# A decoder layer's first projection: two token groups of v and a taken from x without its norm, and the first loads reordered

## Chip, cores and metric

The kernel runs on one core of a Trainium2 chip. The metric is device time in microseconds; a time is the median of several executions. One execution was also taken with the hardware profiler, and all rows shown here come from it.

## The reference, cut to what matters

One layer of a decoder over 512 tokens of 1024 features, all in float32:

```python
h = rms_norm(x, g_mix)                 # x * rsqrt(mean(x*x) + eps) * g
proj = h @ w_in                        # (512, 1024) @ (1024, 3088)
q, k, v, g, a_low, B, C, u = split(proj)    # 256, 256, 512, 512, 16, 512, 512, 512 columns
...                                    # gated linear attention, short convolution
x = x + concat(A, B) @ w_out
x = x + hier_moe(rms_norm(x, g_moe))   # 16 experts, two of them per token
x = x + sigmoid(rms_norm(x, g_ple) @ w_ple_gate) * (p @ w_ple_proj)
return rms_norm(x, g_final)
```

What matters here is the product that gives v (512 columns) and a_low (16 columns). The norm divides each row of x by one number, so `rms_norm(x) @ w` equals `r * ((x * g) @ w)`, where r is that row's reciprocal root mean square: the factor may be applied to the rows of the product.

## The kernel before, in words

**Precision.** A float32 product is made of three products of rounded operands. A matrix is split into a high part (`hi`, `hTh`), rounded by ScalarE (ACT) as it copies, and a low part (`lo`, `hTl`), the remainder, formed by VectorE (DVE). TensorE (PE) then adds up high x high, high x low and low x high. So each weight tile and each tile of activations passes ACT, then DVE, before its last matmul.

**Weights.** `Stream` (line 53) keeps a list of weight blocks to be loaded (`specs`), a few load buffers (`raw0` to `raw2` here), and split tiles. `load` (line 83) issues the DMAs of the next block on SyncE's queue (SP) where a buffer is free. `split` (line 103) queues the high parts on ACT (line 117, scaled by the gain g_mix, which comes as the columns of `cst`) and the low parts on DVE (line 118); with `later=True` the low parts are handed back as a function and are queued where that is called. `give` frees the buffer when the last low part is queued, and that queues the next load. One block has 512 rows of w_in as four k tiles of 128 rows. The blocks for v and a have 528 columns, 512 wide ones and 16 narrow ones, which are two DMAs.

**Work of the first stage.** Tokens are four groups (t) of 128; features are eight k tiles of 128, in two halves (i) of four. Per group: `norm_in(t)` (line 328) squares half 0 on ACT and half 1 on DVE, adds them on DVE, and takes the power -0.5 on GpSimd (POOL), line 238; `scale_in(t)` (line 332) multiplies half 0 on ACT and half 1 on DVE by the result; `tr_half(t, i)` (line 337) transposes four 128 x 128 blocks on PE into PSUM (line 341), copies them to `hTh` on ACT (line 344), and forms `hTl` on DVE (line 345); `va_mm` (line 373) runs six matmuls of 264 columns per k tile (line 378); `va_out` (line 381) copies v and a out of PSUM on ACT and DVE. The next stage, the q|k projection (`proj_steps`, line 442, matmuls on line 454), reads `hTh` and `hTl` of all four groups.

**Order.** The schedule is written out by hand: each engine runs its instructions in the order in which the Python code queues them, and waits at the head of its queue for what it needs. Before the stage, dummy matmuls (`warm`, line 314) run on PE. Lines 400 to 440 are the order of the stage; in it group 0 is normed, scaled and transposed before its first matmul:

```python
    norm_in(0)
    copy_cst()
    scale_in(0)
    tr_half(0, 0)()
    W.pump(1)
```

**Loads.** SP issues x of group 0 (two halves of 256 KB), then the first weight block in two parts (each 512 KB wide and 8 KB narrow, shown as 16.0 KB by the profile), x of group 1, the second block likewise, x of groups 2 and 3, small rows, and the third block. g_mix is loaded on ACT's queue.

Of the kernel before, what the change touches and what calls it, by code (L numbers as in the profile page):

```python
# [13 lines left out]
AF = mybir.ActivationFunctionType  # L14
OP = mybir.AluOpType
# [6 lines left out]
NT = S // P  # L22
NK = D // P
# [29 lines left out]
class Stream:  # L53
# [26 lines left out]
            self.free.append(at)  # L80
        self.load()

    def load(self, n=99, parts=1, eng=None):
        eng = eng or self.nc.sync
        while n and self.free and self.specs:
            n -= 1
            spec = self.specs.pop(0)
            if callable(spec):
                spec()
                continue  # L90
            src, r0, nk, c0, cn, c1, c1n, gain = spec
            w = cn + c1n
            at, raw = self.slot(nk * w)
            v = raw.rearrange("p (k c) -> p k c", k=nk)
            rows = src[r0:r0 + nk * P, :].rearrange("(k p) c -> p k c", p=P)
            for i in range(parts):
                ks = slice(nk // parts * i, nk // parts * (i + 1))
                eng.dma_start(v[:, ks, :cn], rows[:, ks, c0:c0 + cn])
                if c1n:
                    eng.dma_start(v[:, ks, cn:], rows[:, ks, c1:c1 + c1n])  # L100
            self.loaded += [(raw, nk // 2, w, 0, None, gain), (raw, nk // 2, w, 1, at, gain)]

    def split(self, hi=None, lo=None, eng=None, later=False):
        eng = eng or self.nc.vector
        raw, n, w, i, at, gain = self.loaded.pop(0)
        if hi is None:
            hi = self.hl.tile([P, n * w], F32R, tag="hi", name="hi")
            lo = self.hl.tile([P, n * w], F32R, tag="lo", name="lo")
        rw = raw[:, n * w * i:n * w * (i + 1)]
        los = []  # L110
        if gain is None:
            self.nc.scalar.copy(hi, rw)  # L112
            los.append(lambda: eng.tensor_sub(lo, rw, hi.bitcast(F32)))  # L113
        else:
            for j in range(n):
                c_, g_ = slice(j * w, (j + 1) * w), gain[:, n * i + j:n * i + j + 1]
                self.nc.scalar.activation(hi[:, c_], rw[:, c_], AF.Copy, scale=g_)  # L117
                los.append(lambda c_=c_, g_=g_: eng.scalar_tensor_tensor(  # L118
                    lo[:, c_], rw[:, c_], g_, hi[:, c_].bitcast(F32), op0=OP.mult, op1=OP.subtract))
        self.ready.append([(hi[:, j * w:(j + 1) * w], lo[:, j * w:(j + 1) * w]) for j in range(n)])  # L120

        def rest(n=9):
            for _ in range(min(n, len(los))):
                los.pop(0)()
            if not los and at is not None:
                self.give(at)

        if later:
            self.live += 1
            return rest  # L130
        rest()

    def pump(self, n=1, eng=None):
# [18 lines left out]
def hymba_layer(ctx, tc, x, p, g_mix, w_in, w_gla_gate, b_gla_gate, g_gla_out, w_conv, w_out,  # L152
# [3 lines left out]
    x, out = x[0], out[0]  # L156
    p, w_in, w_out = p[0, 0], w_in[0], w_out[0]
    ve, se, pe, ge, sy = nc.vector, nc.scalar, nc.tensor, nc.gpsimd, nc.sync
    ctx.enter_context(tc.manual_schedule())

    def pool(stack, name, bufs, **kw):
        return stack.enter_context(tc.tile_pool(name=name, bufs=bufs, **kw))
# [3 lines left out]
    ring = pool(ctx, "ring", 1)  # L166
# [7 lines left out]
    def mm_ps(name):  # L174
        return ps.tile([P, HALF], F32, tag="mm", name=name)

    def aux_ps(name):
        return psa.tile([P, HALF], F32, tag="aux", name=name)

    def half(i):  # L180
        return slice(i * HALF, (i + 1) * HALF)

    def tok(t):
        return slice(t * P, (t + 1) * P)


    W = Stream(nc, hlp, 6)
# [8 lines left out]
    def X(t):  # L196
        return xt[t // 2][:, (t % 2) * D:(t % 2 + 1) * D]

    ident = consts.tile([P, P], F32, name="ident")
# [4 lines left out]
    cst = consts.tile([P, 40], F32, name="cst")  # L204
# [3 lines left out]
    later = consts.tile([P, 5, 4, 4], U8, name="later")  # L208
# [44 lines left out]
    def t2k(name, dt=F32):  # L253
        return t2.tile([P, HALF], dt, tag="t2", name=name)

    def txk(name, dt=F32):
        return tx.tile([P, HALF], dt, tag="tx", name=name)
# [8 lines left out]
    for ci in range(2):  # L266
        add_columns(w_out, HALF * ci)

    def load_x(t):
        for i in range(2):  # L270
            sy.dma_start(X(t)[:, half(i)], x[tok(t), half(i)])

    load_x(0)
    rows = t2k("rows")[:, :P]
    wg = mc.tile([RANK, 256], F32, name="wg")
    ve.memset(rows, 0.0)
# [1 line left out]
    def load_row(eng, r0, vec):  # L278
        n = vec.shape[-1] // P
        eng.dma_start(rows[r0:r0 + n, :], vec[0].rearrange("(k p) -> k p", p=P))  # L280

    load_row(se, 0, g_mix)
    se.preload_act_table_set("natural_log_exp_and_others")
    W.free += [(ring, f"raw{i}") for i in range(3)]
    W.load(1, 2)
    load_x(1)
    W.load(1, 2)
    load_x(2)
    load_x(3)
    for r0, vec in ((8, b_gla_gate), (10, g_gla_out), (23, g_moe), (31, g_ple)):  # L290
        load_row(sy, r0, vec)
    sy.dma_start(rows[11:23, :], w_conv[0].rearrange("j (i p) -> (j i) p", p=P))
# [7 lines left out]
    def small_loads():  # L300
        ge.dma_start(wr[:, :, 0:4], w_group[0].rearrange("(k p) c -> p k c", p=P))
        ge.dma_start(wr[:, :, 4:20], w_router[0].rearrange("(k p) c -> p k c", p=P))
        bcast(brt[:, 0:4], b_group[0], 4)
        bcast(brt[:, 4:20], b_router[0], 16)
        bcast(gmoe, g_moe[0], D)
# [3 lines left out]
    def make_cst(a, b_):  # L309
        pt = aux_ps(f"pt_rows{a}")  # L310
        pe.transpose(pt[:, :b_], rows[:b_, :], ident[:b_, :b_])
        return lambda: se.copy(cst[:, a:b_], pt[:, a:b_])

    def warm(n, pw):

        for _ in range(n):
            pe.matmul(pw[:, :P], ones, ones, start=True, stop=True)

    pw = mm_ps("pw")

    def fold_gain():
        for k in range(NK):
            ge.tensor_scalar(wr[:, k, :], wr[:, k, :], cst[:, 23 + k:24 + k], None, op0=OP.mult)


    xn, rin = {}, {}

    def norm_in(t):
        xn[t] = junk = [txk(f"xn{t}_{i}") for i in range(2)]
        rin[t] = norm_rows(X(t)[:, :], junk, f"mix{t}")  # L330

    def scale_in(t):
        junk, r = xn[t], rin[t]
        se.mul(junk[0], X(t)[:, half(0)], r)
        ve.tensor_scalar(junk[1], X(t)[:, half(1)], r, None, op0=OP.mult)

    def tr_half(t, i):

        pk = aux_ps(f"pk{t}_{i}")
        for k in range(4):  # L340
            pe.transpose(pk[:, tok(k)], xn[t][i][:, tok(k)], ident)
        pv = pk.rearrange("p (k t) -> p k t", k=4)
        dh, dl = hTh[:, 4 * i:4 * i + 4, tok(t)], hTl[:, 4 * i:4 * i + 4, tok(t)]
        se.copy(dh, pv)
        return lambda: ve.tensor_sub(dl, pv, dh.bitcast(F32))

    def tr_in(t):
        for i in range(2):
            tr_half(t, i)()
# [21 lines left out]
    at_ = [mc.tile([P, RANK], F32, name=f"at{t}") for t in range(NT)]  # L371

    def va_mm(t, pp, ks):
        for k in ks:
            wh, wl = va[k]
            for n, (a, b_) in enumerate(((hTh, wh), (hTh, wl), (hTl, wh))):
                for i in range(2):
                    pe.matmul(pp[i][:, :264], a[:, k, tok(t)], b_[:, i * 264:(i + 1) * 264],
                              start=(k + n == 0), stop=(k == NK - 1 and n == 2))

    def va_out(t, pp):
        v_ = t2k(f"v{t}")
        ve.tensor_copy(at_[t], pp[1][:, 248:264])
        se.copy(v_[:, :264], pp[0][:, :264])
        ve.tensor_copy(v_[:, 264:], pp[1][:, :248])
        vt.append(v_)

    def a_tr(t, pa):
# [1 line left out]

    pp = {}

    def va_half(t, i):
        if i == 0:
            pp[t] = [mm_ps(f"va{t}_{j}") for j in range(2)]
        va_mm(t, pp[t], range(4 * i, 4 * i + 4))
        if i:
            va_out(t, pp[t])

    warm(6, pw)  # L400
    copy_cst = make_cst(0, 8)
    warm(6, pw)
    norm_in(0)
    copy_cst()
    scale_in(0)
    tr_half(0, 0)()
    W.pump(1)
    lo = W.split(later=True)
    lo(1)
    norm_in(1)  # L410
    lo(1)
    lo = tr_half(0, 1)
    scale_in(1)
    lo()
    va = W.take() + W.take()
    va_half(0, 0)
    tr_in(1)
    norm_in(2)
    va_half(1, 0)
    W.pump(1)  # L420
    scale_in(2)
    W.pump(1)
    va += W.take() + W.take()
    tr_in(2)
    va_half(0, 1)
    norm_in(3)
    scale_in(3)
    va_half(1, 1)
    tr_in(3)
    make_cst(8, 39)()  # L430
    small_loads()
    make_masks()
    va_half(2, 0)
    va_half(2, 1)
    fold_gain()
    W.pump(2)
    va_half(3, 0)
    va_half(3, 1)
    make_routing()
    W.done(4)  # L440

# [598 lines left out]
    t = NT - 1  # L1040
# [451 lines left out]
    for t in range(NT):  # L1492
        n = t + 1
# [15 lines left out]
    t = NT - 1  # L1509
# [29 lines left out]
    r = small.tile([P, 1], F32, tag="rstd", name="rs_last")  # L1539
# [33 lines left out]
```

## Time and profile before

| what | us |
|---|---|
| median of 3 runs | 609.72 (609.4 to 611.09) |
| the profiled execution, its own time | 609.15 |
| its span, first to last instruction | 607.4 |
| PE, DVE, ACT, POOL busy | 587.7, 481.6, 365.3, 113.6 |
| stage of v and a, first matmul to the q pass's first weight load | 8.76 to 38.84 |

Times in rows are microseconds from the span's start, durations of one instruction often in ns. PE is the matmul row, PEld the weight loads beside it. SPq and ACTq are DMA issues on those queues. L378 is line 378 of the kernel, and it may be a helper's line. A matmul's shown duration has its pipeline's length in it, so the pitch of a series is read from starts. An instruction's row says in brackets how long its engine was idle before it and what released it.

### The profile page before, as it was taken

The page shows a single profiled execution, that of the slowest core. Times are in us where ns is not written, and L with a number is a line of the kernel's source. Part 1 is how long each engine was busy: PE and PEld are TensorE (multiplying, and loading weights), DVE is VectorE, ACT ScalarE, POOL GpSimd, SP SyncE. Part 2 cuts the span into 40 slices and gives each one's busy share as a digit, 9 for nine tenths or more (in the row PEclk, how much of TensorE's full clock was granted, in tenths as well). Part 3 has the DMA queues.
Part 4 walks back from the last instruction along what each step waited for, and adds up shares of the span by engine and source line. Part 5 has one row for each costly group of instructions (what it writes and reads, how often), then busy time and mean ns, then how long its engine had stood idle before and what let it go on. Part 6 is the DMA issues. An engine that isn't in the chain of part 4 may idle for free.

```text
span 607.4 us, 8456 instructions
## 1 busy us (share of the span) xinstructions
PE 587.7 (97%) x3026; PEld 450.6 (74%) x3026; DVE 481.6 (79%) x814; ACT 365.3 (60%) x520; POOL 113.6 (19%) x148
## 2 busy tenths in 40 slices
PE   7999999999999999899999999999999999989995
PEld 6997888887687788677777777777777777666884
DVE  4742799874396476799999999999999999879764
ACT  5532537303715333768877878877787898776232
POOL 1440664100420000123210222220122210000101
PEclk9999999999999999999999999999999999999998
DMA  8732222221126958599999999999999999992001
GB/s 282 215 105 71 70 70 69 70 73 68 42 96 215 389 210 306 197 376 369 373 371 371 365 369 367 388 379 364 362 341 365 377 344 380 373 366 99 36 35 70
DMA packets 65324, 148.62 MB, mean 245 GB/s; under 512 B 4747, under 2 KB 5346, under 8 KB 65262
## 3 DMA queue, kind: packets, MB, share of 16 engines
q1 hardware_dynamic: 61374, 136.69, 60.9%
q0 software_dynamic: 3744, 11.09, 8.0%
q8 instruction: 24, 0.39, 0.3%
q10 hardware_dynamic: 160, 0.27, 0.1%
q14 instruction: 22, 0.18, 0.1%
HBM read 137.56 MB, written 12.71 MB: 247 GB/s over the span
## 4 chain that ended last, share of the span: by engine, by line
PE 52%; DVE 4%; ACT 2%; issue 1%; POOL 0%; DVEq 0%; POOLq 0%; ACTq 0%
PE pg L1125 14%; PE pd L1125 14%; PE pu L1125 13%; PE pgate L1125 5%; PE pt_xT L1113 2%; DVE lo L113 1%; PE pgate_last L1526 1%; PE pt_hT L1113 1%; DVE lo L118 1%; ACT hi L112 1%; PE px L1432 1%; PE pz L1260 0%; PE pslot L938 0%; ACT L1396 0%; ACT ye L1319 0%
## 5 line engine op out<-in xcount | busy, mean ns | idle before, releaser
L113 DVE TENSOR_TENSOR lo<-raw,hi 128x1024 fp32r<-128x1024 f32 x172 | 203.5, 1218 | 13.3 <-ACT hi L112 12.1
L112 ACT CAST hi<-raw 128x1024 fp32r<-128x1024 f32 x172 | 170.8, 1052 | 2.5 <-DMA raw<-in_w_exp_down_dram 1.7
L1095 POOL DMA_INDIRECT xe<-xgd,toki x16 | 27.0, 1685 | 190.5 <-PE pt_xT L1113 164.5
L118 DVE SCALAR_TENSOR_TENSOR lo<-raw,cst,hi 128x512 fp32r<-128x512 f32 (+1 forms) x56 | 44.7, 842 | 16.2 <-ACT hi L117 16.0
L113 DVE TENSOR_TENSOR lo<-x,hi 128x1024 fp32r<-128x1024 f32 x30 | 36.0, 1218 | 1.0 <-ACT hi L112 0.8
L117 ACT ACTIVATE hi<-raw,cst 128x512 fp32r<-128x512 f32 (+1 forms) x56 | 36.6, 717 | 0.0
L1146 POOL DMA_INDIRECT xd<-ye,rowi x15 | 22.9, 1525 | 48.6 <-ACT ye L1319 44.9
L112 ACT CAST hi<-x 128x1024 fp32r<-128x1024 f32 x30 | 30.9, 1052 | 0.0
L1125 PE MATMUL pg<-hi,xT_1h 128*96 128x512 f32 x60 | 24.3, 406 | 0.0
L1125 PE MATMUL pg<-hi,xT_0l 128*96 128x512 f32 x60 | 23.8, 396 | 0.0
L1125 PE MATMUL pg<-hi,xT_0h 128*96 128x512 f32 x60 | 23.8, 396 | 0.0
L1125 PE MATMUL pg<-lo,xT_0h 128*96 128x512 f32 x60 | 23.7, 395 | 0.0
L1125 PE MATMUL pg<-hi,xT_1l 128*96 128x512 f32 x60 | 23.6, 394 | 0.0
L1125 PE MATMUL pg<-lo,xT_1h 128*96 128x512 f32 x60 | 23.6, 393 | 0.0
L1125 PE MATMUL pu<-hi,xT_0h 128*96 128x512 f32 x56 | 22.7, 405 | 0.0
L1125 PE MATMUL pu<-hi,xT_1l 128*96 128x512 f32 x56 | 22.2, 396 | 0.0
L1125 PE MATMUL pu<-hi,xT_0l 128*96 128x512 f32 x56 | 22.2, 396 | 0.0
L1125 PE MATMUL pu<-hi,xT_1h 128*96 128x512 f32 x56 | 22.1, 394 | 0.0
L1125 PE MATMUL pu<-lo,xT_1h 128*96 128x512 f32 x56 | 22.1, 394 | 0.0
L1125 PE MATMUL pu<-lo,xT_0h 128*96 128x512 f32 x56 | 22.0, 393 | 0.0
L645 ACT ACTIVATE sq<-xs 128x512 f32<-128x512 f32 x4 | 2.5, 632 | 28.5 <-DVE xs L627 28.5
L737 POOL TENSOR_TENSOR xs<-xs,sg 128x128 f32<-128x128 f32 x16 | 11.3, 738 | 44.2 <-ACT sg L732 44.1
(584 smaller groups left out, 1588.6 us busy)
## 6 DMA issues: line engine op xcount, KB each, us to landing
raw<-in_w_exp_gate_dram SPq DMA_DIRECT2D x28, 1024.0 KB, 16.9
raw<-in_w_exp_down_dram SPq DMA_DIRECT2D x27, 1024.0 KB, 16.1
raw<-in_w_exp_up_dram SPq DMA_DIRECT2D x26, 1024.0 KB, 15.7
raw<-in_w_in_dram SPq DMA_DIRECT2D x10, 1024.0 KB, 5.0
x<-in_w_exp_up_dram SPq DMA_DIRECT2D x6, 1024.0 KB
x<-in_w_exp_down_dram SPq DMA_DIRECT2D x5, 1024.0 KB, 16.4
xs<-in_x_dram SPq DMA_DIRECT2D x16, 256.0 KB, 5.8
raw<-in_w_out_dram SPq DMA_DIRECT2D x4, 1024.0 KB
```

The costliest lines, as they stand in the source:

```text
L112: self.nc.scalar.copy(hi, rw)
L113: los.append(lambda: eng.tensor_sub(lo, rw, hi.bitcast(F32)))
L117: self.nc.scalar.activation(hi[:, c_], rw[:, c_], AF.Copy, scale=g_)
L118: los.append(lambda c_=c_, g_=g_: eng.scalar_tensor_tensor(lo[:, c_], rw[:, c_], g_, hi[:, c_].bitcast(F32), op0=OP.mult, op1=OP.subtract))
L645: se.activation(osq[c], to[c], AF.Square)
L737: ge.tensor_tensor(tv, tv, sgs[i][:, tok(t)], op=OP.mult)
L1095: ge.indirect_dma_start(out=x_, out_offset=None, in_=xgd, in_offset=bass.IndirectOffsetOnAxis(ap=idx, axis=0), bounds_check=S - 1, oob_is_ ...
L1113: pe.transpose(pt[:, k * n:(k + 1) * n], src[:n, tok(k)], ident[:n, :n])
L1125: pe.matmul(dst, a, b_, start=(k + n == 0), stop=(k == nk - 1 and n == 2))
L1146: ge.indirect_dma_start(out=xd, out_offset=bass.IndirectOffsetOnAxis(ap=idx, axis=0), in_=y_, in_offset=None, bounds_check=S + P - 1, oob_ ...
L1432: pe.transpose(pt[:, tok(k)], X(t)[:, ci * HALF + k * P:ci * HALF + (k + 1) * P], ident)
L1526: pe.matmul(pgl[i][:, :256], a, b_[:, 256 * i:256 * i + 256], start=(k + n == 0), stop=(k == NK - 1 and n == 2))
```

## The change

It has four parts.

1. For token groups 0 and 1, x itself is transposed (`tr_raw`), split, and multiplied with the gained weights. `va_out` multiplies the rows of v and a by r as it copies them out of PSUM. The normed and scaled groups 0 and 1 are still transposed later (`tr_in(0)`, `tr_in(1)`), since q, k and all other projections read them.
2. The two weight blocks are split k tile by k tile (`steps=True`: the high parts are handed back as functions too), and the order of matmuls is by k tile instead of by half (`va_k` for `va_half`).
3. The loads: x by halves, weights in four parts of 256 KB wide columns, the narrow columns of a block in two DMAs ahead of its wide ones; those of the first block on ACT's queue. Order on SP: x0 half 0, block 0, x1 half 0, x0 half 1, block 1, x1 half 1, groups 2 and 3, and then as before.
4. The copies of `cst` go from ACT to DVE. The dummy matmuls are eight before the first transposes and six after, for six and six. `make_cst(8, 39)`, `small_loads`, `make_masks` and `fold_gain` come later in the order.

The diff, cut:

```diff
     def load(..., narrow=None):
+            for n1 in range(2 * bool(c1n)):
+                ks = slice(nk // 2 * n1, nk // 2 * (n1 + 1))
+                (narrow or eng).dma_start(v[:, ks, cn:], rows[:, ks, c1:c1 + c1n])
             for i in range(parts):
                 eng.dma_start(v[:, ks, :cn], rows[:, ks, c0:c0 + cn])
-                if c1n:
-                    eng.dma_start(v[:, ks, cn:], rows[:, ks, c1:c1 + c1n])
...
-    W.load(1, 2)
-    load_x(1)
-    W.load(1, 2)
-    load_x(2)
-    load_x(3)
+    W.load(1, 4, narrow=se)
+    se.preload_act_table_set("natural_log_exp_and_others")
+    load_x(1, 0)
+    load_x(0, 1)
+    W.load(1, 4)
+    load_x(1, 1)
+    for t in range(2, NT):
+        for i in range(2):
+            load_x(t, i)
...
-        return lambda: se.copy(cst[:, a:b_], pt[:, a:b_])
+        return lambda: ve.tensor_copy(cst[:, a:b_], pt[:, a:b_])
...
+    def tr_raw(t, i):
+        return tr_half(t, i, X(t)[:, half(i)])
...
     def va_out(t, pp):
+        if t < 2:
+            r = rin[t]
+            ve.tensor_scalar(at_[t], pp[1][:, 248:264], r, None, op0=OP.mult)
+            se.mul(v_[:, :264], pp[0][:, :264], r)
+            ve.tensor_scalar(v_[:, 264:], pp[1][:, :248], r, None, op0=OP.mult)
...
+    warm(8, pw)
+    xlo = tr_raw(0, 0)
+    copy_cst = make_cst(0, 8)
+    copy_cst()
     warm(6, pw)
+    xlo()
+    (h0, l0), (h1, l1) = W.split(steps=True), W.split(steps=True)
+    va = W.take() + W.take()
+    for f in h0 + h1:
+        f()
+    l0(1)
+    va_k(0, 0)
+    l0(1)
+    va_k(0, 1)
+    xlo = tr_raw(1, 0)
+    l1(1)
+    va_k(0, 2)
+    xlo()
+    va_k(1, 0)
+    l1(1)
+    va_k(1, 1)
+    va_k(0, 3)
+    xlo = tr_raw(0, 1)
+    va_k(1, 2)
+    (h0, l0), (h1, l1) = W.split(steps=True), W.split(steps=True)
+    va += W.take() + W.take()
+    for f in h0:
+        f()
+    xlo()
+    l0(1)
+    va_k(1, 3)
+    l0(1)
+    va_k(0, 4, 5)
+    xlo = tr_raw(1, 1)
+    for f in h1:
+        f()
+    xlo()
+    l1(1)
+    norm_in(0)
+    va_k(0, 6)
+    va_k(1, 4)
+    l1(1)
+    va_k(1, 5)
+    va_k(0, 7)
+    norm_in(1)
+    va_k(1, 6)
+    norm_in(2)
+    va_k(1, 7)
+    scale_in(2)
+    tr_in(2)
+    scale_in(0)
+    va_k(2, 0, 1, 2)
+    norm_in(3)
+    tr_in(0)
+    scale_in(3)
+    va_k(2, 3, 4)
+    scale_in(1)
+    make_cst(8, 39)()
+    tr_in(3)
+    small_loads()
+    va_k(2, 5, 6, 7)
+    tr_in(1)
     make_masks()
     fold_gain()
+    va_k(3, 0, 1)
     W.pump(2)
+    va_k(3, 2, 3, 4, 5, 6, 7)
     make_routing()
```

## Rows read from the trace of the kernel before

**Rows 1.** The page, part 1: busy time, share of the span, instructions of PE.

```profile
PE 587.7 (97%) x3026; PEld 450.6 (74%) x3026; DVE 481.6 (79%) x814; ACT 365.3 (60%) x520; POOL 113.6 (19%) x148
```

**Rows 2.** Windows: stretch and length, busy us of each engine, PEclk, DMA, GB/s.

```profile
8.76:38.84 30.08, 27.98 (x217) 26.36 (x217) 19.55 (x48) 15.61 (x31) 14.18 (x41) 1.00 0.62 201
...
38.84:60.00 21.16, 21.16 (x89) 15.46 (x88) 6.54 (x11) 5.99 (x11) 0.00 (x0) 1.00 0.28 96
```

**Rows 3.** Timeline of PE in the head: start, us, instruction, idle before.

```profile
1.27 2.93 PE L317 MATMUL pw<-ones 128*128 128x128 f32 x12 [1.27 <-DVE ones L297]
...
2.07 1.06 PE L317 MATMUL pw<-ones 128*128 128x128 f32 x4
...
2.92 1.06 PE L317 MATMUL pw<-ones 128*128 128x128 f32 x4
...
8.76 0.51 PE L378 MATMUL va<-hi,hTh 128*128 128x264 f32 x2 [0.87 <-ACT hi L117]
...
19.09 1.09 PE L341 MATMUL pk<-ident,xn 128*128 128x128 f32 x8 [0.69 <-ACT xn L334]
...
19.94 0.49 PE L378 MATMUL va<-hi,hTh 128*128 128x264 f32 x2
...
27.17 0.51 PE L378 MATMUL va<-hi,hTh 128*128 128x264 f32 x2
...
38.84 0.19 PEld L454 LDWEIGHTS qk<-hTh,hi 128*128 128x128 f32 x1
```

**Rows 4.** Timeline of ACT, DVE and PE: the links of the chains.

```profile
7.97 2.62 ACT L117 ACTIVATE hi<-raw,cst 128x528 fp32r<-128x528 f32 x4
...
8.74 2.13 DVE L118 SCALAR_TENSOR_TENSOR lo<-raw,cst,hi 128x528 fp32r<-128x528 f32 x3
...
9.57 0.50 PE L378 MATMUL va<-lo,hTh 128*128 128x264 f32 x2 [0.29 <-DVE lo L118]
...
10.49 0.62 ACT L232 ACTIVATE xn<-xs 128x512 f32<-128x512 f32 x1
...
11.59 0.16 DVE L236 SCALAR_TENSOR_TENSOR msmix<-s2mix 128x1 f32<-128x1 f32 x1
...
12.88 0.72 ACT L334 ACTIVATE xn<-xs,rsmix 128x512 f32<-128x512 f32 x1 [1.21 <-POOL rsmix L238]
...
13.66 1.09 PE L341 MATMUL pk<-ident,xn 128*128 128x128 f32 x8 [0.41 <-ACT xn L334]
...
14.35 1.07 ACT L344 CAST hTh<-pk 128x512 fp32r<-128x512 f32 x2 [0.75 <-PE pk L341]
...
14.97 1.29 DVE L345 TENSOR_TENSOR hTl<-pk,hTh 128x512 fp32r<-128x512 f32 x2 [1.00 <-ACT hTh L344]
...
23.03 0.38 ACT L384 COPY v<-va 128x264 f32<-128x264 f32 x1 [1.78 <-PE va L378]
```

**Rows 5.** Loads: issues, first uses of x, SP's wait, issue to landing of x1.

```profile
1.10 0.59 ACTq L280 DMA_DIRECT2D rows<-in_g_mix_dram  x1
...
3.52 0.63 ACT L232 ACTIVATE xn<-xs 128x512 f32<-128x512 f32 x1 [0.52 <-DMA xs<-in_x_dram]
...
3.73 1.23 SPq L271 DMA_DIRECT2D xs<-in_x_dram  x2
...
4.30 0.69 DVE L233 SCALAR_TENSOR_TENSOR xn<-xs 128x512 f32<-128x512 f32 x1 [3.09 <-DMA xs<-in_x_dram]
...
6.96 0.37 SPq L98 DMA_DIRECT2D raw<-in_w_in_dram  x1
...
SPq L98 <- DMA raw<-in_w_in_dram: 0.7, 1, 0.7
...
xs<-in_x_dram SPq DMA_DIRECT2D x2, 256.0 KB, 5.8
```

**Rows 6.** Windows at the kernel's end: PE has no more work, then PEclk.

```profile
600.00:602.60 2.60, 0.00 (x0) 0.00 (x0) 1.44 (x5) 0.47 (x1) 0.39 (x1) 1.00 0.00 0
602.60:607.40 4.80, 0.00 (x0) 0.00 (x0) 0.75 (x2) 0.72 (x1) 0.16 (x1) 0.51 0.29 111
```

More of the change, by code (lines that the diff above doesn't have):

```diff
@@ L81, in give, with load @@
         self.load()
-    def load(self, n=99, parts=1, eng=None):
+    def load(self, n=99, parts=1, eng=None, narrow=None):
         eng = eng or self.nc.sync
@@ L98, in load, with split @@
                 eng.dma_start(v[:, ks, :cn], rows[:, ks, c0:c0 + cn])
-                if c1n:
-                    eng.dma_start(v[:, ks, cn:], rows[:, ks, c1:c1 + c1n])
             self.loaded += [(raw, nk // 2, w, 0, None, gain), (raw, nk // 2, w, 1, at, gain)]
-    def split(self, hi=None, lo=None, eng=None, later=False):
+    def split(self, hi=None, lo=None, eng=None, later=False, steps=False):
         eng = eng or self.nc.vector
@@ L109, in split @@
         rw = raw[:, n * w * i:n * w * (i + 1)]
-        los = []
+        los, his = [], []
         if gain is None:
@@ L116, in split @@
                 c_, g_ = slice(j * w, (j + 1) * w), gain[:, n * i + j:n * i + j + 1]
-                self.nc.scalar.activation(hi[:, c_], rw[:, c_], AF.Copy, scale=g_)
+                his.append(lambda c_=c_, g_=g_: self.nc.scalar.activation(hi[:, c_], rw[:, c_], AF.Copy, scale=g_))
+                if not steps:
+                    his.pop()()
                 los.append(lambda c_=c_, g_=g_: eng.scalar_tensor_tensor(
@@ L126, in rest @@
                 self.give(at)
-        if later:
+        if later or steps:
             self.live += 1
-            return rest
+            return (his, rest) if steps else rest
         rest()
@@ L267, in hymba_layer, with load_x @@
         add_columns(w_out, HALF * ci)
[L269 to L273, printed above, removed]
+    def load_x(t, i):
+        sy.dma_start(X(t)[:, half(i)], x[tok(t), half(i)])
+    load_x(0, 0)
     rows = t2k("rows")[:, :P]
@@ L282, in hymba_layer @@
     load_row(se, 0, g_mix)
+    W.free += [(ring, f"raw{i}") for i in range(3)]
+    W.load(1, 4, narrow=se)
     se.preload_act_table_set("natural_log_exp_and_others")
-    W.free += [(ring, f"raw{i}") for i in range(3)]
-    W.load(1, 2)
-    load_x(1)
-    W.load(1, 2)
-    load_x(2)
-    load_x(3)
+    load_x(1, 0)
[5 more added lines that the diff above has]
+            load_x(t, i)
     for r0, vec in ((8, b_gla_gate), (10, g_gla_out), (23, g_moe), (31, g_ple)):
@@ L335, in scale_in, with tr_half @@
         ve.tensor_scalar(junk[1], X(t)[:, half(1)], r, None, op0=OP.mult)
-    def tr_half(t, i):
+    def tr_half(t, i, src=None):
         pk = aux_ps(f"pk{t}_{i}")
+        src = xn[t][i] if src is None else src
         for k in range(4):
-            pe.transpose(pk[:, tok(k)], xn[t][i][:, tok(k)], ident)
+            pe.transpose(pk[:, tok(k)], src[:, tok(k)], ident)
         pv = pk.rearrange("p (k t) -> p k t", k=4)
@@ L382, in va_out @@
         v_ = t2k(f"v{t}")
-        ve.tensor_copy(at_[t], pp[1][:, 248:264])
-        se.copy(v_[:, :264], pp[0][:, :264])
-        ve.tensor_copy(v_[:, 264:], pp[1][:, :248])
+        if t < 2:
[3 more added lines that the diff above has]
+            ve.tensor_scalar(v_[:, 264:], pp[1][:, :248], r, None, op0=OP.mult)
+        else:
+            ve.tensor_copy(at_[t], pp[1][:, 248:264])
+            se.copy(v_[:, :264], pp[0][:, :264])
+            ve.tensor_copy(v_[:, 264:], pp[1][:, :248])
         vt.append(v_)
@@ L391, in hymba_layer, with va_k @@
     pp = {}
[L393 to L398, printed above, removed]
-    warm(6, pw)
-    copy_cst = make_cst(0, 8)
-    warm(6, pw)
-    norm_in(0)
-    copy_cst()
-    scale_in(0)
[L406 to L412, printed above, removed]
+    def va_k(t, *ks):
+        for k in ks:
+            if k == 0:
+                pp[t] = [mm_ps(f"va{t}_{j}") for j in range(2)]
+            va_mm(t, pp[t], (k,))
+            if k == NK - 1:
+                va_out(t, pp[t])
+    warm(8, pw)
+    xlo = tr_raw(0, 0)
+    copy_cst = make_cst(0, 8)
+    copy_cst()
+    warm(6, pw)
+    xlo()
[31 more added lines that the diff above has]
+    l1(1)
+    norm_in(0)
+    va_k(0, 6)
[9 more added lines that the diff above has]
+    tr_in(2)
+    scale_in(0)
+    va_k(2, 0, 1, 2)
[3 more added lines that the diff above has]
+    va_k(2, 3, 4)
     scale_in(1)
-    lo()
-    va = W.take() + W.take()
-    va_half(0, 0)
+    make_cst(8, 39)()
+    tr_in(3)
+    small_loads()
+    va_k(2, 5, 6, 7)
     tr_in(1)
[L418 to L431, printed above, removed]
     make_masks()
-    va_half(2, 0)
-    va_half(2, 1)
     fold_gain()
+    va_k(3, 0, 1)
     W.pump(2)
-    va_half(3, 0)
-    va_half(3, 1)
+    va_k(3, 2, 3, 4, 5, 6, 7)
     make_routing()
```

## The prediction

> **What bounds the kernel now.** The page comes first: TensorE (PE) is busy 97% of the span [rows 1]. An average says nothing of one stage, so next come the windows: from 38.84 us on PE has no idle time, through the next 21 us and on; in 8.76 to 38.84 us, the stage that makes v and a (va below), it is busy 27.98 of 30.08 us, and the other engines 14 to 20 [rows 2]. So PE carries the end, and what the change does to the time is how far it moves the moment at which the q|k projection begins, with its first weight load at 38.84 us [rows 3]. What follows runs on PE's work and should move with it.
>
> The timeline of PE gives the prices [rows 3]. The dummy matmuls run at a slow pace at first: four instructions between 2.07 and 2.92 us, 0.213 each. Transposes later: eight in 0.85 us, 0.107 each, just half. The va matmuls: 96 between 27.17 and 38.84, 0.1215 each, so one k step (six) is 0.73. From the first va matmul at 8.76 the stage is 192 x 0.1215 = 23.33, 24 transposes (2.57), one of 39 rows (0.2), which is 26.1; the other 3.98 of the 30.08 us are waits, start to start.
>
> The timeline of ACT, DVE and PE together gives the links of a chain, start to start [rows 4]: a half's transposes to its copy 0.69, copy to low part 0.62, two copies 1.07; a weight's high part 0.66 each on ACT, high to its matmul 0.79 (7.97 to 8.76), high to low 0.77, low 0.71 each, low to its matmul 0.83; square to mean 1.10, mean to scaling 1.29 (POOL's power lies between), scaling to transpose 0.78; the v copy on ACT 0.38.
>
> **The change, part by part.**
>
> *Start.* Eight dummy matmuls (16 instructions at 0.213, for the twelve of six now) from 1.27 [rows 3] end at 4.68; x's first half landed by 3.52 [rows 5]; four transposes and the eight-row one end near 5.6; six dummies at the fast pace, 12 x 0.115, end at 7.0. Beside it ACT copies hTh at 5.70 (0.38 after the fourth transpose, which starts at 5.32) and makes the high parts from 6.22, so the dummies are the last to be done and the first va matmul starts at 7.02 instead of 8.76: **-1.74**.
>
> *More transposes.* After its first va matmul the old order has 24, the new one 12 raw and 32 normal: 20 x 0.107 = **+2.14**. Nothing hides them; PE is the bound.
>
> *Loads.* DMAs move in queue order. In the old order 0.5 MiB (x0) had landed at 4.30, where the square of its second half starts; 1.0 MiB (and k0, k1) at 6.96, where SP's next issue ends its 0.7 us wait for a weight load; 1.75 MiB (and k2, k3, half of x1) at 3.73 + 5.8 = 9.53 [rows 5]. By bytes, the new order has k0 at 4.3, k1 at 5.6, k2 7.0, k3 7.8, x1's first half 8.7, x0's second 9.5, k4 10.3 and so on at 0.7 to 0.8. ACT wants k0 at 6.22, k2 at 7.53, k3 at 8.18; PE wants x1 at 9.0: none is late, by 0.3 at the closest. One microsecond later costs 0.5, two cost 1.5; earlier gains nothing. Eighteen SP issues for 16, at under 0.5 each, are hidden behind the transfers; two narrow issues go to ACT, where one took 0.59, and push its table load by 1.2; ACT sat idle 0.52 before 3.52, so it is ready by 4.2, before 5.70. The small rows and the next weights move some microseconds back behind them; the q|k stage, 20 us on, covers them. [...] Here halves of 256 KB, issued within 1.23 us, both took 5.8 us to land, so they overlap, and I keep the bytes.
>
> *Waits of the new order.* Walked queue by queue, each engine in program order with the links above, PE waits here:
> - 7.25, the low part of k0. High part 6.22, low 6.22 + 0.77 = 7.0, its matmul 7.83: 0.58.
> - 10.2, token group 1's first half. Its transposes stand on PE after k1, at 9.04; copy 9.73, first matmul 10.36, low part and its matmul 0.75 later. PE's only cover is one k step (9.47 to 10.20): 0.16, then 0.26 after two pairs of matmuls.
> - 14.7, k4. ACT queues its high part behind the copy of x0's second half, whose transposes stand at 12.81 on PE. Copy 13.51, high part 14.03, its matmul 14.81; low part 14.81, its matmul 15.64. PE has two k steps of group 1 for cover, to 14.70: 0.12 + 0.59.
> - **17.3, k6.** Its high part stands on ACT behind the copy of group 1's second half, whose transposes (16.86) stand on PE just ahead of the k6 matmuls. 16.86 + 0.69 + 0.52 + 0.79 = 18.86, low part 18.86, its matmul 19.69; PE was free at 17.29 and has nothing between: 1.57 + 0.59. Faster loads don't help; k6 landed near 12.
> - **23.8, the normed group 2.** Squares for it stand on ACT behind v0's copy and the square of group 1. va of group 0 ends 22.35; copy from 22.55, 0.3; square 1, 0.71 (its 0.62 and the read of its sum); square 2 to mean 1.10; scaling 1.29; transposes 0.78: 26.7. PE has two k steps, 1.46 us, and is free at 23.82: 2.86.
> - 27.5, matmuls right behind group 2's eight transposes: copy 0.69 after their start at 26.68, matmul 0.62 on, 28.0, low part again later: 0.47 + 0.26. And 0.27 at 33.4, for group 3's scaling.
>
> The sum is 7.73 for 3.98: **+3.75**.
>
> *The rest.* Scaling in the v copies, on PSUM sources, isn't in the trace: at least nothing (same elements, one operand more, so no gain) and at most 0.18 a copy (0.72 for scaling 512 columns less 0.54, half of 1.07, for copying them [rows 4]); I take zero; it could add 0.1 to the 2.86. The cst copy on DVE instead of ACT: DVE idles there. Small loads, masks and routing constants start some 7 us later: POOL's 14.2 us of work in the stage [rows 2] then ends in the q|k window, which covers them. Behind the mask steps DVE queues the low parts of q|k, due one per k step of twelve matmuls, 2.9 us by the 89 in 21.16 us [rows 2].
>
> *Sum.* -1.74 + 2.14 + 3.75 = 4.15: q|k starts at 43.0. The same walk over the old order ends 0.14 late, so I take **+4.0**. The profiled execution took 609.15 us (span 607.4), 0.57 under the median of 609.72: 613.15 against the one, **613.7** as a median. Links a tenth shorter would take 0.7 off, loads a microsecond late add 0.5: 612.5 to 614.7.
>
> **Rivals.** A measurement can tell 0.3%, 1.83 us, from no change.
>
> *The clock falls in the long wait: 615.6.* The clock stood at full for 2.6 us after the last matmul of the kernel and at 0.51 in the rest [rows 6]. Between group 1's last va matmul (23.8) and group 2's first (28.0) PE has only eight transposes. At half clock (1.2 GHz) matmuls take twice as long, as the dummies at the head did [rows 3]; if the fall comes at 26.5 and 4 us run so, 2 us of work is lost, 0.1 of it in time that PE would have waited: +1.9. For it: that row. Against: the transposes may count as activity. The Trainium skill, "TensorE: Matmul & The Clock Gate", Part 4, says that transposes don't count as busy in the way matmuls do; that speaks for this rival, and no run here shows it.
>
> *The waits are covered: faster, 607.1.* Place: PE from 7 to 37 us. Work without waits ends at 7.02 + 28.24 = 35.3. If the other engines run ahead of PE as they do from 27.17 on, where it never waits, and 1 us is left, q|k starts at 36.3, -2.6. It decides where the waits sum to under 1.75. For: DVE and ACT are busy only 65% and 52% of the stage [rows 2]. Against: the chains at 17.3 and 23.8 alone are 5.0, and both are the order on one queue, not load.
>
> *The delay is taken up later: 610.5, no change.* A later wait on something that didn't move would absorb 3 of the 4 us. For: the chain isn't shown from the head to the end without a gap. Against: no idle PE in the next 21 us [rows 2], and weight loads are started by freed buffers, which move too.
>
> **How the numbers follow.** Forecast 0.51, clock 0.27 (both slower: 0.78), covered 0.09, taken up 0.13. The range, 610.8 to 616.8, holds forecast and clock with late loads, and the upper part of the third; what is left out is the faster case, half of the unchanged one, and 0.04 above.
>
> **What would show it.** First va matmul near 7.0; PE waits on ACT and DVE near 17 (2.1) and before group 2's transposes (2.9); 48 full transposes by 43 us; q|k starting near 42.8, and everything after it shifted by that and no more. Matmuls twice as long from 26.5 would show the clock. A q|k start before 39 would make me wrong; so would waits on DMA in the first 13 us over 1 us, in a step of mine if not in sign.

## Result: 0.7% slower, and the profile after

| | before | after |
|---|---|---|
| median, us | 609.62 (609.34 to 611.09, 6 runs) | 614.53 (613.21 to 614.97, 6 runs) |
| ratio, 95% interval | | 1.0069 [1.006, 1.0079] |
| profiled execution, us | 609.15 | 614.97 |
| first va matmul, us | 8.76 | 7.57 |
| q\|k stage's first weight load, us | 38.84 | 44.71 |

The change costs 4.9 us in the median and 5.82 us between the two profiled executions. The page of the changed kernel answers to [rows 1]:

```profile
PE 591.6 (96%) x3046; PEld 454.4 (74%) x3046; DVE 484.5 (79%) x820; ACT 367.1 (60%) x522; POOL 113.0 (18%) x148
```

PE has 20 instructions more, as the change has it: 20 transposes. Its busy time grew by 3.9 us, which is more than twenty transposes make. Its share fell all the same, so PE also stood idle for longer.

The windows of the changed kernel (stretch and length, busy us of PE, PEld, DVE, ACT, POOL, then PEclk, DMA share, GB/s) say where:

```profile
7.57:44.71 37.14, 32.21 (x236) 30.19 (x237) 23.26 (x56) 19.21 (x37) 14.71 (x42) 0.95 0.53 171
23.00:28.80 5.80, 3.07 (x24) 2.62 (x23) 3.53 (x12) 3.89 (x10) 1.45 (x2) 1.00 0.63 246
28.85:32.26 3.41, 3.41 (x17) 3.33 (x16) 2.04 (x6) 1.27 (x4) 1.18 (x2) 0.50 0.00 0
...
44.71:613.20 568.49, 553.51 (x2779) 418.69 (x2777) 460.02 (x761) 345.23 (x482) 97.50 (x98) 1.00 0.70 247
```

And the one window of the kernel before that answers to the last of them:

```profile
38.84:607.40 568.56, 553.51 (x2779) 418.71 (x2777) 459.76 (x760) 345.54 (x482) 98.12 (x98) 1.00 0.70 247
```

Read the last rows first. From the q|k stage's first weight load to the end, both kernels take the same time within 0.07 us, with the same 553.51 us of PE. So the whole difference lies ahead of that load: it comes 5.87 us later. The stage of v and a is 37.14 us long against 30.08 [rows 2], and in 28.85 to 32.26 us PE's granted clock is 0.50, the lower of its two levels (1.2 GHz).

PE's waits in 6.9 to 45 us of the changed kernel (what waits, for what: us in total, times, longest):

```profile
PE pk L347 <- ACT xn L339: 2.5, 1, 2.5
PE va L388 <- ACT hi L118: 1.7, 2, 1.3
PE va L388 <- DVE lo L121: 0.9, 3, 0.3
PE va L388 <- ACT hTh L350: 0.2, 1, 0.2
```

Two waits stand out, and the timeline of PE gives both their places (L388 is the va matmul, L347 the transpose, L499 the q|k matmul):

```profile
7.57 0.51 PE L388 MATMUL va<-hi,hTh 128*128 128x264 f32 x2 [0.38 <-ACT hi L118]
8.37 0.51 PE L388 MATMUL va<-lo,hTh 128*128 128x264 f32 x2 [0.30 <-DVE lo L121]
...
17.53 0.60 PE L347 MATMUL pk<-ident,xs 128*128 128x128 f32 x4
19.44 0.51 PE L388 MATMUL va<-hi,hTh 128*128 128x264 f32 x2 [1.31 <-ACT hi L118]
20.24 0.51 PE L388 MATMUL va<-lo,hTh 128*128 128x264 f32 x2 [0.30 <-DVE lo L121]
20.59 0.41 PE L388 MATMUL va<-hi,hTl 128*128 128x264 f32 x2
...
24.23 0.40 PE L388 MATMUL va<-hi,hTl 128*128 128x264 f32 x2
27.13 1.09 PE L347 MATMUL pk<-ident,xn 128*128 128x128 f32 x8 [2.49 <-ACT xn L339]
28.46 0.51 PE L388 MATMUL va<-hi,hTh 128*128 128x264 f32 x2 [0.24 <-ACT hTh L350]
...
30.23 0.64 PE L388 MATMUL va<-lo,hTh 128*128 128x264 f32 x2
30.67 0.64 PE L388 MATMUL va<-hi,hTl 128*128 128x264 f32 x2
...
32.36 1.04 PE L347 MATMUL pk<-ident,xn 128*128 128x128 f32 x8
...
44.71 0.19 PEld L499 LDWEIGHTS qk<-hTh,hi 128*128 128x128 f32 x1
```

The shown idle is smaller than the real one, since a pair's shown end has the pipeline's length in it. From start to start the 8.37 pair comes 0.80 after its predecessor, where a pair takes 0.24: a wait of 0.56, not 0.30. Behind 28.85 the pairs start 0.44 apart (30.23, 30.67) instead of 0.24: that is the clock at 0.50, as a busy PE shows it.

The timeline of ACT, with DVE's last mean, shows what made PE wait in the two places, and why the stage didn't begin at 7.02:

```profile
6.78 2.62 ACT L118 ACTIVATE hi<-raw,cst 128x528 fp32r<-128x528 f32 x4 [0.65 <-DMA raw<-in_w_in_dram]
...
18.16 0.58 ACT L350 CAST hTh<-pk 128x512 fp32r<-128x512 f32 x1 [2.18 <-PE pk L347]
18.64 1.36 ACT L118 ACTIVATE hi<-raw,cst 128x528 fp32r<-128x528 f32 x2
...
23.16 0.48 ACT L396 ACTIVATE v<-va,rsmix 128x264 f32<-128x264 f32 x1 [2.54 <-PE va L388]
23.54 0.62 ACT L235 ACTIVATE xn<-xs 128x512 f32<-128x512 f32 x1
...
24.16 0.62 ACT L235 ACTIVATE xn<-xs 128x512 f32<-128x512 f32 x1
...
25.50 0.16 DVE L239 SCALAR_TENSOR_TENSOR msmix<-s2mix 128x1 f32<-128x1 f32 x1
...
26.35 0.72 ACT L339 ACTIVATE xn<-xs,rsmix 128x512 f32<-128x512 f32 x1
```

ACT idles 2.18 us for PE's transposes before 18.16 and 2.54 us for PE's matmuls before 23.16. Behind the copies that wait there stand, in its queue, the high parts of k6 and the squares of group 2, whose own inputs had long been there. Then PE waits for those in turn. That is a wait passed to and fro between two engines, each with work that could have been done. The first row is the high part of k0: it waits for a load, until 6.78.

The profiled difference adds up: start 7.57 - 8.76 = -1.19; twenty transposes +2.14; the stage's 37.14 us less its work of 28.24 is 8.90, of which 1.34 is the clock (from group 2's first matmul to the next transposes 3.90 us, 28.46 to 32.36; 2.56 at full clock, in the first experiment below); the other 7.56 are waits, against 3.98 before: +3.58. The sum is 5.87.

### The profile page after: what moved, and what is told of

Read it like the earlier page. It is cut to its first block, busy times and chain, and to the rows that moved or that the text cites. A ratio compares the mean times of both kernels' runs of the same rounds, so it can differ in the third digit from the quotient of the medians.

```text
span 613.2 us, 8511 instructions
## 1 busy us (share of the span) xinstructions
PE 591.6 (96%) x3046; PEld 454.4 (74%) x3046; DVE 484.5 (79%) x820; ACT 367.1 (60%) x522; POOL 113.0 (18%) x148
## 4 chain that ended last, share of the span: by engine, by line
PE 52%; DVE 4%; ACT 1%; issue 1%; POOLq 0%; DVEq 0%; ACTq 0%
PE pg L1170 14%; PE pd L1170 14%; PE pu L1170 13%; PE pgate L1170 5%; PE pt_xT L1158 2%; DVE lo L114 1%; PE pgate_last L1571 1%; PE pt_hT L1158 1%; DVE lo L121 1%; ACT hi L113 1%; PE px L1477 1%; PE pz L1305 0%; PE pslot L983 0%; ACT L1441 0%; DVE vals L1048 0%
## 5 line engine op out<-in xcount | busy, mean ns | idle before, releaser
L1364 ACT ACTIVATE ye<-pd,sw 96x512 f32<-96x512 f32 x30 | 19.0, 683 | 0.9 <-PE pd L1170 0.9
```

The lines of the kernel that those rows point to most:

```text
L1364: se.activation(y_[:, half(ci)], pds[ci][:CAP], AF.Copy, scale=sw[:, e, 0:1])
```

## Experiments

Two theories were set against each other. *Order*: the time goes into the two waits that the queues' order makes, and into the transposes. *Clock*: what the waits cost is mainly PE's clock. A third question was the loads. Kernels on one chip share their runs of the kernel before: e1 to e4 (609.45 us), e5 to e8 (609.51), e9 to e11 (609.69). The change itself ran beside e5 to e8 only, as e5, so the medians of the others are set against its 614.53 across chips; its own two medians, 614.53 and 615.54, are 1.0 apart. All edits are to the changed kernel.

**e1_dummies: PE is kept at work in the long wait.**

```diff
     va_k(1, 7)
+    warm(9, mm_ps("pw2"))
     scale_in(2)
```

> The changed kernel with nine dummy matmuls (18 instructions, 1.9 us) put on PE into the wait ahead of token group 2's transposes; nothing else. Theory A (the order on the queues makes the waits, and the longest wait drops PE's clock): the granted clock stays at 1.00 through the stage, the 2.5 us wait shrinks to about 0.6 but the transposes start where they did (27.1), the va matmuls behind them keep the 0.1215 us pitch, and the q|k projection starts at 43.0 instead of 44.7; median 613.2, 1.3 below the change. Rival B (the clock's fall has nothing to do with the wait): it falls all the same, q|k at 44.7, 614.5. Rival C (the loss is the extra transposes and the loads): the clock may stay, and the time hardly moves.

Measured: 614.73 us (612.87 to 615.9), ratio 1.0082 [1.0067, 1.0097]. The timeline of PE in its profile:

```profile
25.01 2.17 PE L322 MATMUL pw<-ones 128*128 128x128 f32 x18
27.65 1.09 PE L347 MATMUL pk<-ident,xn 128*128 128x128 f32 x8 [0.48 <-ACT xn L339]
28.98 0.51 PE L388 MATMUL va<-hi,hTh 128*128 128x264 f32 x2 [0.24 <-ACT hTh L350]
```

The dummies fill 2.17 us of the wait, the clock reads 1.00 through the whole stage, and q|k starts at 43.88, 0.83 earlier than in the change, although the first va matmul is 0.52 later. Yet the median, forecast at 613.2, isn't below the change's 614.53, as far as medians of two chips can say. So the profile bears out what the fall costs in this place (0.83 + 0.52 = 1.35), and the median suggests that this place isn't all: the five executions without a profile spread over 612.9 to 615.9 us with a mean granted clock of 0.993 to 0.998, and what happened in them isn't seen. That a gain in the median was missing here is why e5 and e6 were run.

**e2_weights_early: the high and low parts of k4 to k7 are queued earlier,** each pair one half's transposes ahead: k4 and k5 behind the first copy of group 1, k6 and k7 behind that of x0's second half.

```diff
     xlo = tr_raw(1, 0)
+    (h2, l2), (h3, l3) = W.split(steps=True), W.split(steps=True)
+    va += W.take() + W.take()
+    for f in h2:
+        f()
...
     xlo = tr_raw(0, 1)
+    l2(1)
+    for f in h3:
+        f()
     va_k(1, 2)
-    (h0, l0), (h1, l1) = W.split(steps=True), W.split(steps=True)
```

> The changed kernel with the high and low parts of the second weight block queued earlier: k4 and k5 behind group 1's first copy, k6 and k7 behind the copy of x0's second half, each low part ahead of the low part of x that it stood behind. Theory A: the waits at k4 (0.3) and k6 (1.3 and 0.3) go, the wait ahead of group 2's transposes stays at 2.5 and moves 1.9 earlier; q|k starts at 42.8 if the clock falls in that wait and 41.1 if not; median 611.3 to 612.6. Rival C (the waits only pass on what the loads or PE's own work set): the waits come back behind, q|k stays above 44.

Measured: 612.58 us (612.06 to 613.24), ratio 1.0047 [1.0034, 1.006]. PE's waits in 6.9 to 42.5 us:

```profile
PE pk L347 <- ACT xn L339: 2.5, 1, 2.5
PE va L388 <- ACT hi L118: 0.7, 1, 0.7
PE va L388 <- DVE lo L121: 0.3, 1, 0.3
```

What is left of the waits for high and low parts is the start (first va matmul at 8.04). The waits for k4 and k6 are gone, and q|k starts at 42.38, 2.33 earlier than in the change from a start 0.47 later: 2.80. That is the 0.71 and 2.16 us that the walk had for k4 and k6 together (2.87). The clock still fell, to 0.50 in 25.76 to 29.17, behind the wait that this edit left.

**e3_norm2_early: the squares and scalings of group 2 are queued earlier.**

```diff
     va_k(0, 4, 5)
+    norm_in(2)
     xlo = tr_raw(1, 1)
...
     va_k(1, 5)
+    scale_in(2)
     va_k(0, 7)
     norm_in(1)
     va_k(1, 6)
-    norm_in(2)
     va_k(1, 7)
-    scale_in(2)
     tr_in(2)
```

> The changed kernel with the norm of group 2 put ahead of group 1's second raw transposes, and its scaling ahead of the last k step of group 0. Theory A: the 2.5 us wait ahead of group 2's transposes goes, some 1 us of it comes back behind them (copy and low part right ahead of the matmuls); the clock stays at 1.00; the waits at k4 and k6 stay; q|k starts at 41.0 to 41.6, median 611 to 611.7. Rival B: the clock falls anyway, 1.7 more. Rival C: PE waits elsewhere, q|k above 43.

Measured: 613.81 us (611.26 to 614.77), ratio 1.0069 [1.0055, 1.0083]. The profiled execution is the one of 611.26. PE's waits there, in 6.9 to 41.1 us:

```profile
PE va L388 <- ACT hi L118: 1.5, 2, 1.3
PE va L388 <- ACT hTh L350: 0.9, 1, 0.9
PE va L388 <- DVE lo L121: 0.9, 3, 0.3
```

The 2.5 us are gone, 0.7 of them come back as a longer wait for group 2's copy, the clock reads 1.00, and q|k starts at 41.01: 3.70 earlier than in the change (0.37 from the start, 1.34 from the clock, the other 1.99 from the waits), and this execution is 3.71 shorter than the change's. But that is this execution; the median, forecast at 611 to 611.7, is 2.6 us above it. **e11_norm2_early_again**, the same kernel on another chip, was run to see where the others lose it:

> The third experiment's kernel (norm of group 2 early) for a second look, since five of its six executions had a mean clock of 0.990 to 0.993 and took 612.3 to 614.8, where the profiled one had 0.997 and took 611.3. Theory A: its wait at k6 (1.3 and 0.3 us, transposes ahead of it) drops the clock in most executions, as it did in the second look at the change; if this profile catches one, PEclk is 0.50 for 3.4 us from 21 to 22 us on, and q|k starts 1.5 to 3 us later than 41.1. Rival: the clock falls in a stretch without a wait.

Measured: 613.47 us (613.38 and 613.56), ratio 1.0057 [1.0037, 1.0077]. A window of its profile:

```profile
21.65:25.06 3.41, 3.41 (x18) 3.41 (x18) 1.00 (x2) 0.10 (x1) 1.03 (x1) 0.50 1.05 408
```

Here the clock fell behind the 1.3 us wait for k6, which this edit leaves. First va matmul 8.08, q|k 43.37: 2.36 later than in e3, of which 0.88 is the start and the other 1.48 about one fall.

**e4_both_early: both, and group 2's transposes in halves around group 1's last k step.** The same instructions in another order. Besides e2's edit it holds the one below, and further down the square of group 3 and the scaling of group 1 stand earlier, and one k step of group 2 ahead of group 3's transposes:

```diff
     va_k(0, 4, 5)
+    norm_in(2)
     xlo = tr_raw(1, 1)
...
     va_k(1, 4)
-    l1(1)
+    scale_in(2)
+    va_k(0, 7)
     va_k(1, 5)
-    va_k(0, 7)
     norm_in(1)
     va_k(1, 6)
-    norm_in(2)
+    tr_half(2, 0)()
     va_k(1, 7)
-    scale_in(2)
-    tr_in(2)
+    tr_half(2, 1)()
```

> Both reorderings at once, with the same instructions as the changed kernel: weights' parts early, norm of group 2 early, its two half transposes around the last k step of group 1, scalings of groups 0 and 3 earlier. Theory A: hardly a wait left after the first k steps (some 2.0 us in all against 6.2), clock 1.00, q|k starts at 37.4 to 38.2, ahead of the 38.84 of the kernel before; median 608.4 to 609.1. Rival C: 20 transposes more than before (2.1 us) against a start 1.2 us earlier can't come out below before; median 610.5 or more.

Measured: 608.35 us (607.29 to 608.73, 11 runs), ratio 0.9977 [0.9968, 0.9985]: 1.1 us below the kernel before on the same chip, and 6.2 below the change by the medians of two chips. PE's waits in 6.9 to 37.2 us are one line:

```profile
PE va L388 <- DVE lo L121: 0.2, 1, 0.2
```

The windows of the same profile:

```profile
7.00:37.00 30.00, 29.70 (x239) 28.58 (x238) 23.26 (x55) 19.32 (x37) 13.43 (x37) 1.00 0.66 216
37.00:58.00 21.00, 21.00 (x89) 15.33 (x88) 6.97 (x13) 5.77 (x10) 1.19 (x6) 1.00 0.31 101
```

And its first weight load of q|k:

```profile
37.09 0.19 PEld L500 LDWEIGHTS qk<-hTh,hi 128*128 128x128 f32 x1
```

PE is busy 29.70 of 30.00 us at full clock, with the same transposes as in the change. The first va matmul is at 7.03 and q|k starts at 37.09: 1.75 earlier than before, and this execution is 1.86 shorter than that of before. Here the change's own plan shows: start -1.73, transposes +2.14, and waits of 1.82 instead of 3.98 by the count used above (30.06 less 28.24).

**e5_change_again: the change once more,** on the chip of the next three.

> The changed kernel itself once more, on the same chip as the three kernels beside it, for a second look at its clock and for a median to compare them with. Theory A: the first va matmul at 7.0 to 8.1, the waits at 2.1 and 2.5 us as in the first profile; the clock may fall behind the second or not (q|k at 44.7 or 43.0); median 614.0 to 614.8, its executions in two heaps 1.5 us apart.

Measured: 615.54 us (614.2 to 616.39), ratio 1.0087 [1.0074, 1.01], above the 614.0 to 614.8 that were expected. Two windows of its profile, the longest of its executions:

```profile
21.97:25.39 3.42, 3.42 (x18) 3.42 (x17) 0.46 (x1) 0.21 (x1) 0.87 (x1) 0.50 1.05 408
28.80:32.20 3.40, 2.96 (x13) 2.74 (x14) 1.19 (x3) 1.93 (x4) 0.00 (x0) 0.50 0.00 0
```

The clock fell twice, once behind each of the two waits. The first va matmul came at 8.26 and q|k at 46.20: 1.49 later than in the first profile of this kernel, 0.69 of it from the start; the other 0.80 goes with the second fall.

**e6_dummies_twice: dummies in both waits.**

```diff
     xlo = tr_raw(1, 1)
+    warm(5, aux_ps("pw3"))
     for f in h1:
...
     va_k(1, 7)
+    warm(9, mm_ps("pw2"))
```

> The first experiment's nine dummy matmuls ahead of group 2's transposes, and five more (10 instructions, 1.1 us) in the wait at k6. Theory A': what the first dummies didn't mend is a fall of the clock from the other wait in some executions; then with both filled the clock stays at 1.00 in all of them, q|k starts at 43.0 to 44.0, and the median is 0.8 to 1.5 below the change run beside it. Rival D (the executions differ in when the clock first rises, at the head, and the waits have little to do with it): the median stays within 0.5 of the change.

Measured: 614.10 us (613.2 to 614.62), ratio 1.0067 [1.0054, 1.008], 1.44 below e5 (the two intervals overlap by a little). The clock is 1.00 through the stage in its profile, and its mean was 0.996 or more in four of five executions. That mean doesn't rule a fall out: it also holds the stretch of some 2 to 5 us at half clock at the kernel's end (4.80 us at 0.51 in [rows 6]), and one fall of 3.4 us is worth some 0.003 of it. The dummies do no work and shorten no chain, so what they give is the clock: about one fall. All the rest of the loss, 4.6 us over the kernel before, stays. So the clock is a part of it, near 1.4 us by the medians (an estimate, as only one execution of each was profiled), and the order and the transposes are the larger part.

**e7_no_second_transposes: the 16 transposes of normed groups 0 and 1 are left out,** with their copies and low parts.

```diff
     norm_in(3)
-    tr_in(0)
     scale_in(3)
...
     va_k(2, 5, 6, 7)
-    tr_in(1)
     make_masks()
```

> The changed kernel without the second transposes of groups 0 and 1 (16 on PE, 4 copies on ACT, 4 low parts on DVE): q, k and all later projections then read those two groups of x without the norm's factor, which is left out of the computation. Theory A: the transposes lie on PE with nothing to hide them, so q|k starts 16 x 0.107 = 1.7 us earlier at the same clock, and the median is 1.5 to 2.0 below the change run beside it. Rival: ACT and DVE set the pace behind 28 us, and without their copies it is more than 2.5.

Measured: 613.88 us (613.03 to 615.42), ratio 1.0068 [1.0054, 1.0081], 1.66 below e5. Its timeline of PE, where q|k starts:

```profile
43.37 0.19 PEld L497 LDWEIGHTS qk<-hTh,hi 128*128 128x128 f32 x1
```

Against the change's 44.71, from a start 0.49 later (8.06) and with one clock fall as there, that is 1.83 for 16 transposes; 16 x 0.107 makes 1.71. They are paid in full, nothing hides them.

**e8_old_loads: the loads in the order and sizes of before,** except that a block's narrow columns still go ahead of its wide ones.

```diff
     load_x(0, 0)
+    load_x(0, 1)
...
-    W.load(1, 4, narrow=se)
+    W.load(1, 2)
     load_x(1, 0)
-    load_x(0, 1)
-    W.load(1, 4)
     load_x(1, 1)
+    W.load(1, 2)
```

> The changed kernel with the loads in the order of before: both halves of x0, the first block in two parts with its narrow pieces on SP, both halves of x1, the second block likewise. Theory A: k0 and its narrow piece are there by 7.0 to 7.4, where the new order had them at 6.8; the first va matmul is 0.2 to 0.6 later, group 1's first half lands at 9.5, just in time; all later waits are the same, the median within 0.6 of the change run beside it. Rival (the new loads are the gain at the start): first va matmul at 8.5 or later, the median 1 us or more above.

Measured: 615.59 us (614.12 to 615.72), ratio 1.0087 [1.0074, 1.01]: the change's own time beside it. Its timeline of ACT:

```profile
7.26 2.62 ACT L118 ACTIVATE hi<-raw,cst 128x528 fp32r<-128x528 f32 x4 [1.41 <-DMA raw<-in_w_in_dram]
```

The first high part at 7.26 is between the change's two (6.78 and 7.47 in e5). So the new order of the loads, the piece of the change that was to feed the earlier start, brings nothing that shows in the change's order of the queues. With few waits left, as in e4, the old loads weren't tried.

**e9_narrow_first and e10_both_early_again: can the narrow columns come earlier?** Both are e4; e9 issues the narrow columns ahead of g_mix on ACT's queue.

```diff
-    load_row(se, 0, g_mix)
     W.free += [(ring, f"raw{i}") for i in range(3)]
     W.load(1, 4, narrow=se)
+    load_row(se, 0, g_mix)
```

> The kernel of the fourth experiment with the narrow pieces of the first weight block issued on ACT's queue ahead of g_mix instead of behind it, 0.6 us earlier. Theory A: the start hangs on the narrow pieces (landed 4.9 to 5.3 us after their issue in the change's profile, later than k0's wide part should need), so the first high part starts at 6.2 to 6.5, the first va matmul at 7.0 to 7.3 in every execution; the median is 0.2 to 0.7 below the fourth experiment's kernel beside it. Rival (the wide part of k0 is what comes late): no difference.

> The fourth experiment's kernel again, beside the one with the narrow pieces first, for a comparison on one chip and a second look. Median 608.0 to 608.7, 0.8 to 1.5 under the kernel before; clock at 1.00 from the head to the end of PE's work; first va matmul at 7.0 to 8.1, q|k at 37.2 to 38.3.

Measured: e9 607.64 us (607.56 to 608.03), ratio 0.9963 [0.9949, 0.9977]; e10 608.50 (607.85 to 610.02), ratio 0.9979 [0.9967, 0.999]. Both beat the kernel before, by 2.1 and 1.2 us, so e4's gain holds on a second chip. The first va matmul that was expected of e9, 7.0 to 7.3, didn't come. Which of the two is better stays open: the intervals overlap, both profiles have their first high part at 6.42, and in both the first va matmul (7.87 and 8.06) waited for the dummies ahead of it. The timeline of PE in e10:

```profile
6.04 2.27 PE L322 MATMUL pw<-ones 128*128 128x128 f32 x12
...
8.06 0.49 PE L388 MATMUL va<-hi,hTh 128*128 128x264 f32 x2
```

Twelve dummies took 1.60 in the change; here they took 2.27, since more of them still ran at the slow pace of the first ones (some 0.21 us each, where the later ones take 0.11).

Not tried: the kernel of before, which transposes only normed tokens, with its own queues mended. So it isn't shown how much of e4's gain needs the raw transposes.

## Why the prediction was right, and where its terms were off

The sign and its reason held: 614.53 us against 613.7 forecast, inside the range, and slower by more than a measurement can miss.

- *Start, -1.74: measured -1.19, and less in most other profiles.* The step that was off is the one in *Loads* that finds no load late. It took k0's wide part for what counts and its narrow columns for next to nothing. The first high part ran at 6.78 (7.47 in e5), not at 6.22, and waited for a load. A row of the change's DMA view, 1.8 to 2 us (queue, count, size, us to landing):

```profile
raw<-in_w_in_dram ACTq DMA_DIRECT2D x1, 16.0 KB, 4.9
```

  This piece (16 KB, not the 8 KB that the text on the change gives for it) was issued at 1.76 and landed at 6.66, 0.12 before the high part. The same views for e3, in 1 to 1.5 us (k0's wide part) and 1.5 to 3.3 us (the narrow pieces):

```profile
raw<-in_w_in_dram SPq DMA_DIRECT2D x1, 256.0 KB, 3.1
raw<-in_w_in_dram ACTq DMA_DIRECT2D x2, 16.0 KB, 4.4
```

  In the eight profiles in which ACT waited for this piece (those of the change, e1 to e3, e5 to e7 and e11) the high part starts 0.06 to 0.14 after its landing, wherever that lay from 6.33 to 7.33. k0's wide part, issued at 1.26, landed 3.0 to 3.6 us later, at 4.3 to 4.9, in the eight profiles that show it (the change's own doesn't), near the 4.3 of the forecast. So the narrow columns are what the start waited for; why they land so late stays open. Where they landed by 5.9, in e4 and e10, ACT didn't wait, and in e4 the first va matmul came at 7.03, as forecast. The late start was passed on one for one: 0.56 late at the high part, 0.55 lost at the first va matmul.
- *More transposes, +2.14.* e7 gives 1.83 for 16 of the 20, where the price says 1.71.
- *Waits, 7.73: measured 7.56.* Place by place, start to start, forecast and measured: k0's low part 0.58 and 0.56; group 1's first half 0.42 and 0.24; k4 0.71 and 0.57; k6 2.16 and 2.04; group 2's norm 2.86 and 2.66; behind its transposes 0.73 and 0.59; group 3's scaling 0.27 and none. These make 6.66. Over half of the other 0.9 is a thing that the walk had not: the pair after a stop is followed 0.34 to 0.35 later instead of 0.24 (20.24 to 20.59), at least five times. Links somewhat too long and a restart cost left out nearly cancelled, so the close sum is in part luck. That the two large ones are order on a queue and not load is shown: with the same instructions e2 takes the one for k6 away, e3 the longer one, and e4 both.
- *The scaled v copies at nothing.* The ACT copy of 264 columns took 0.48 (23.16) against 0.38 [rows 4]: the 0.1 that the text allowed.
- *Delay taken up later (0.13).* Refuted by the two windows from the q|k start on, which differ by 0.07 us.
- *Waits covered (0.09).* Refuted for this order; e4 is that rival come true, by an order that makes the cover.
- *The clock falls (0.27).* This rival was priced too low in chance. The fall came in the profile of the change, where it was looked for and 2.3 us later than forecast, over 3.4 us rather than 4, and cost 1.34 us rather than 1.9. Behind the same long wait it came again in the profiles of e2, e5 and e7, and not in e8. The forecast's q|k start was 1.7 us too early because it left out this fall and took the start for 0.55 too good, less 0.17 for waits: 43.0 + 1.34 + 0.55 - 0.17 = 44.72. The median, only 0.8 us off, was closer than that: the profiled execution is the longest of the six, and not every execution has a fall. The argument against, that transposes may count as activity, isn't settled: between 24.47 and 28.46 PE had nothing but eight transposes and the clock fell, and with matmuls in place of the idle time (e1) it stayed, but the transposes were there both times. The Trainium skill, "TensorE: Matmul & The Clock Gate", Part 4, doesn't count transposes as busy in the way matmuls are; the fall fits that, but no run here had transposes in place of the idle time, so the rule itself isn't shown.

## What to carry to other kernels

When a step is moved to the front of a stage written out by hand, walk what it now stands ahead of on each in-order queue: a copy that waits for PE holds back the splits and squares behind it, and PE then waits for those. Queue work whose inputs are there (the next weights' high parts, the next group's squares) ahead of copies that wait: with the same instructions that was worth some 6 us here by the medians of two chips, about 1.4 of it the clock, and turned a loss into a gain. Price a wait on PE with the chance that it takes the clock along.

## What was not expected of the hardware

**The clock fell behind short waits too.** In e5, e8 and e11 it went to 0.50 at 21.97, 21.46 and 21.65 us, behind the wait of 1.3 us for k6 (about 1.5 start to start), ahead of which PE has four transposes and behind which it was busy again; in the change's first profile and in those of e1, e3 and e7, with the same wait, it didn't. Each fall lasted 3.4 us in the rows and cost 1.3 to 1.5 us, and 0.8 where it lay partly in a wait (the second one of e5). So the same kernel has executions 1.5 us apart; two of the change's six are at 613.2 and four at 614.4 to 615.0. That these heaps are falls is likely by their distance, but not shown, as only one of the six was profiled. The kernel before has such executions too, some 1 us apart: ten of its 38 beside these experiments, those with a mean clock of 0.993, took 610.3 to 610.9 us, and those at 0.995 to 0.998 took 609.1 to 609.8. By an estimate, 0.003 of its 608 us are some 3.6 us at half clock, about one fall.

**The dummies at the head pick up speed at a moment that differs.** They run about 0.21 us each at first and 0.11 later. Twelve of them took 1.60 us in the change and in e1 to e8, 2.08 and 2.27 in e9 and e10, and what stood behind them had to wait by as much as 0.7 longer. The granted clock reads 1.00 in these rows, so they don't show it as the cause.

**A load of 16 KB on ACT's queue took 3.6 to 5.8 us to land,** longer than the 256 KB of k0 issued half a microsecond before it on SP's (3.0 to 3.6). Size alone doesn't set it: in the kernel before x's loads of 256 KB took 2.7 to 5.9, and in the change the second block's 16 KB on SP's queue took 2.4. What does stays open.
